# Four-layer HGRN2 / attention / DeltaNet trunk: wide value projection, output transposes off TensorE, joins set apart, norm in pieces

## The chip, the cores and the metric

The kernel runs on one core of a Trainium2 chip. The metric is the device time of one execution in microseconds (us). A profiled execution was taken beside the timed runs; every duration below comes from it. Engines are named as in the profile: PE is TensorE (matmuls; PEld its weight loads), DVE is VectorE, ACT is ScalarE, POOL is GpSimd, SP is the engine whose DMA queue carries nearly all transfers.

## What is computed

A trunk of four layers over 1024 tokens with 1024 features. Each layer normalises x, shifts and scales it by a conditioning vector, projects it, runs a token mixer, gates the result and adds its output projection to x:

```python
for i in range(DEPTH):                      # 4 layers
    shift, scale, gate = split(c @ ada_w[i] + ada_b[i])
    h = rmsnorm(x, norm_g[i]) * (1.0 + scale) + shift
    y = (hgrn2_mixer, swa_mixer, gdn_mixer)[i % 3](h, ...)   # layers 0 and 3 are HGRN2
    x = x + gate * y

def hgrn2_mixer(h, ...):                    # 8 heads of 128
    q, f_pre, i_, z = split(h @ w_in)       # i_ is the value v
    log_f = log(lb + (1 - lb) * sigmoid(f_pre));  k = (1 - lb) * sigmoid(-f_pre);  q = silu(q)
    o = rmsnorm(hgrn2_scan(q, k, i_, log_f), onorm_g)
    return (o * silu(z)) @ w_out

def swa_mixer(h, ...):                      # 16 query heads of 64, 4 key/value heads, window 128
    q, k, v, z = split(h @ w_in);  q, k = rope(rmsnorm(q)), rope(rmsnorm(k))
    return (softmax_with_sink(q @ k.T, window) @ v * silu(z)) @ w_out

def gdn_mixer(h, ...):                      # 16 value heads of 128, 8 query/key heads
    qkv, z, a, b = split(h @ w_in);  q, k, v = split(silu(causal_conv(qkv)))
    u = solve(I + A, ...)                   # per chunk of 64 tokens, unit lower triangular
    return (rmsnorm(scan(...), onorm_g) * silu(z)) @ w_out
```

Everything is fp32. The kernel splits each operand of a projection into a high and a low part and takes three matmuls for each product (high x high, high x low, low x high).

## The kernel before

**Layout.** x is kept feature-major (128 features in the partitions, 8 blocks of them) in two halves of 512 tokens, each 2 MB, in two "x" slots of SBUF. The normed h is kept as hhi and hlo for each half in four "h" slots. A projection whose result is feature-major (`proj_ps` and `outp_ps` in the profile) holds a 128x128 piece of weight in PE and moves 512 tokens past it. One whose result is token-major (`projt_ps`: the values of HGRN2 and q, k, v of the attention layer) holds 128 tokens of h and moves 256 columns of the weight. All go through `mm3`, the three matmuls L204, L205 and L206.

**Weights.** `load_w` issues a 256 KB load on SP's queue into one of 3 raw buffers (L177), casts it to w_hi on ACT (L179) and subtracts to w_lo on DVE (L180), with 4 buffers each.

**Order.** The mixers are written as generators that yield cost numbers. `weave` takes pieces from several streams in the proportion of their costs: the mixing of a head beside the projections of the next one. A scheduler then orders the instructions of each engine by priority; `burst` and `tied` give a group of small matmuls a high priority so that it stands together. Each engine executes its list in that order, so an instruction that waits holds up everything behind it on its engine.

**HGRN2 (layers 0 and 3).** `proj_v` gives the values of two heads at a time, 256 wide. `mix` works for each head and half: products of levels 1, 3 and 5 (`lev_ps`, L1040 for the first two, L1087 for the last), transposes of k (L1104), a scan over four chunks (`o_ps`, `s_ps`), a norm (L1132 on DVE), four PE transposes back to feature-major (`ot_ps`, L1136), the product with the gate silu(z) (L1139 on DVE) and a store to `od` in DRAM. The diagonal 32x32 blocks are copied by POOL (L1081), the others by ACT (L1090). The last head stays in SBUF. Then `out_load` and `out_mm` form the output projection from `od`.

**Attention (layer 1).** Keys and values are projected first, then one group of four query heads after another while the group before is mixed: scores, softmax, transposes of the probabilities (L1368), products with the values (L1374), which follow the transposes of each block of 128 keys.

**DeltaNet (layer 2).** `proj_kq` and `proj_v` pass through a causal convolution: two ACT reads of the PSUM result (L644 copy, L648 scale), three DVE taps (L650), a tanh. `inverse` builds the inverse of the triangular matrices: 16x16 blocks on DVE, then four *joins*, groups of small matmuls into `z_ps` (L811, L819 to L821, L828, L836), each of which waits for the copies of the one before. `scan` and `finish` follow; `finish` brings the outputs to feature-major with a 32x32-block transpose on DVE (L859) and four stores of 64 KB that put the blocks in place (L862).

**Between layers.** `norm_stats` and `norm_apply` make h for the next layer, half by half: per feature block n_t on DVE (L504), hhi on ACT (L505), hlo on DVE (L506). In the attention and DeltaNet layers, x is written to DRAM (`spill_x`, L127) after its norm and read back (`fill_x`, L132) before the output projection, both on SP's queue, 2 MB each; in the HGRN2 layers it stays in its slots.

## Time and profile before

| what | value |
|---|---|
| timed runs | 2688.74, 2692.27 and 2692.0 us; median 2692.0 us |
| the profiled execution | 2695.95 us, span 2694.2 us |
| PE busy | 2609.7 us (97%) |
| DVE busy | 2010.2 us (75%) |
| ACT busy | 1272.9 us (47%) |
| POOL busy | 136.7 us (5%) |
| DMA | 273.29 MB, 101 GB/s over the span |

Busy time of an engine is the union of its instructions' spans; the recorded length of a matmul (about 400 ns for 128x512) overlaps that of the next, so what a matmul costs in a row of matmuls is the distance between two starts. In a row of the profile stand the line, engine, operation, the tile written and the tiles read, the shape and the count; "idle before" is how long the engine had stood still and what released it.

### The profile page before, as it was taken

Reading aid. Unit: us, or ns where it says so; the run is one execution under the profiler, and the core shown is the slowest. Engines: PE = TensorE matmul, PEld = TensorE weight load, DVE = VectorE, ACT = ScalarE, POOL = GpSimd, SP = SyncE. Lnnn points to the kernel's source line nnn. Section 1 sums busy time; section 2 is a strip of 40 time slices with the busy share of each in tenths; the row PEclk is TensorE's granted clock in tenths of the full one; section 3 lists DMA queues with packets and bytes.
Section 4 is the critical chain, followed back from the end, with each engine's and each line's share of the span. In section 5 each row is a group of like instructions: output and inputs, shape, how many; then the busy total and the mean of one; then the engine's idle time right before and its main releaser. Section 6 shows DMA issues by size and latency. Waiting matters only on the chain.

```text
span 2694.2 us, 51458 instructions
## 1 busy us (share of the span) xinstructions
PE 2609.7 (97%) x18927; PEld 2102.4 (78%) x18927; DVE 2010.2 (75%) x5619; ACT 1272.9 (47%) x3268; POOL 136.7 (5%) x352
## 2 busy tenths in 40 slices
PE   8999999999999999999999999999999999999998
PEld 4878878778878777677877777777788878787877
DVE  6776766788687877777988888989876766656575
ACT  4333333444454655454556556666644433333342
POOL 0000100000000000001001101100000000000000
PEclk9999999999999999999999999999999999999999
DMA  6332222344223252333343333333584221111133
GB/s 241 92 93 84 68 79 72 110 137 157 59 87 103 75 158 91 114 98 84 102 115 99 96 105 100 94 97 82 179 254 132 71 60 37 56 51 43 49 118 115
DMA packets 361490, 273.29 MB, mean 101 GB/s; under 512 B 70499, under 2 KB 294166, under 8 KB 361238
## 3 DMA queue, kind: packets, MB, share of 16 engines
q1 hardware_dynamic: 360950, 268.96, 33.9%
q8 instruction: 149, 2.44, 0.4%
q14 instruction: 103, 0.84, 0.1%
q0 software_dynamic: 288, 1.05, 0.1%
HBM read 224.77 MB, written 45.15 MB: 100 GB/s over the span
## 4 chain that ended last, share of the span: by engine, by line
PE 71%; DVE 17%; DMA 5%; ACT 3%; issue 3%; SPq 1%; POOL 0%; DVEq 0%; ACTq 0%; POOLq 0%
PE proj_ps L206 10%; PE proj_ps L205 9%; PE proj_ps L204 9%; PE outp_ps L204 5%; PE outp_ps L205 5%; PE outp_ps L206 5%; DMA ada_w<-in_ada_w_dram 3%; PE projt_ps L204 3%; PE projt_ps L206 3%; PE projt_ps L205 3%; DVE w_lo L180 2%; DVE gd_tb L650 2%; PE pv_ps L1374 1%; DVE ada_acc L413 1%; PE w_ps L890 1%
## 5 line engine op out<-in xcount | busy, mean ns | idle before, releaser
L204 PE MATMUL proj_ps<-hhi,w_hi 128*128 128x512 f32 x1664 | 675.8, 406 | 6.1 <-ACT gd_tb L648 5.9
L206 PE MATMUL proj_ps<-hhi,w_lo 128*128 128x512 f32 x1664 | 679.9, 409 | 0.0
L205 PE MATMUL proj_ps<-hlo,w_hi 128*128 128x512 f32 x1664 | 671.2, 403 | 0.0
L204 PEld LDWEIGHTS proj_ps<-hhi,w_hi 128*128 128x128 f32 x1664 | 315.3, 190 | 59.4 <-ACT gd_tb L648 6.3
L205 PEld LDWEIGHTS proj_ps<-hlo,w_hi 128*128 128x128 f32 x1664 | 314.7, 189 | 59.0 <-issue 2.4
L206 PEld LDWEIGHTS proj_ps<-hhi,w_lo 128*128 128x128 f32 x1664 | 315.0, 189 | 56.1 <-issue 1.0
L179 ACT CAST w_hi<-w_raw 128x512 fp32r<-128x512 f32 x332 | 202.0, 611 | 303.3 <-PE proj_ps L205 188.1
L180 DVE TENSOR_TENSOR w_lo<-w_raw,w_hi 128x512 fp32r<-128x512 f32 x332 | 223.1, 674 | 155.2 <-ACT w_hi L179 129.1
L205 PE MATMUL projt_ps<-w_lo,hhi 128*128 128x256 f32 x896 | 258.7, 291 | 4.7 <-DVE w_lo L180 4.7
L204 PE MATMUL projt_ps<-w_hi,hhi 128*128 128x256 f32 x896 | 257.8, 290 | 0.6 <-ACT w_hi L179 0.6
L206 PE MATMUL projt_ps<-w_hi,hlo 128*128 128x256 f32 x896 | 256.8, 290 | 0.0
L204 PE MATMUL outp_ps<-o_hi,w_hi 128*128 128x512 f32 x576 | 229.2, 400 | 4.7 <-ACT o_hi L1200 3.4
L205 PE MATMUL outp_ps<-o_lo,w_hi 128*128 128x512 f32 x576 | 229.4, 399 | 0.0
L206 PE MATMUL outp_ps<-o_hi,w_lo 128*128 128x512 f32 x576 | 226.8, 396 | 0.7 <-DVE w_lo L183 0.7
L205 PEld LDWEIGHTS projt_ps<-w_lo,hhi 128*128 128x128 f32 x896 | 171.1, 192 | 8.1 <-DVE w_lo L180 6.0
L204 PEld LDWEIGHTS projt_ps<-w_hi,hhi 128*128 128x128 f32 x896 | 171.1, 192 | 3.7 <-ACT w_hi L179 1.0
L206 PEld LDWEIGHTS projt_ps<-w_hi,hlo 128*128 128x128 f32 x896 | 170.8, 192 | 2.4 <-issue 1.0
L650 DVE SCALAR_TENSOR_TENSOR gd_tb<-gd_xs,taps,gd_tb 128x512 f32<-128x512 f32 x192 | 145.2, 756 | 28.3 <-ACT gd_tb L648 19.7
L182 ACT ACTIVATE w_hi<-w_raw,par 128x512 fp32r<-128x512 f32 (+1 forms) x136 | 94.3, 698 | 137.0 <-PE outp_ps L205 89.2
L204 PEld LDWEIGHTS outp_ps<-o_hi,w_hi 128*128 128x128 f32 x576 | 108.8, 189 | 29.1 <-ACT o_hi L1200 4.9
L413 DVE SCALAR_TENSOR_TENSOR ada_acc<-ada_w,par,ada_acc 128x512 f32<-128x512 f32 x140 | 104.8, 749 | 33.4 <-DMA ada_w<-in_ada_w_dram 32.5
L206 PEld LDWEIGHTS outp_ps<-o_hi,w_lo 128*128 128x128 f32 x576 | 108.7, 189 | 23.5 <-DVE w_lo L183 1.3
(398 smaller groups left out, 4894.8 us busy)
## 6 DMA issues: line engine op xcount, KB each, us to landing
ada_w<-in_ada_w_dram SPq DMA_DIRECT2D x160, 256.0 KB, 2.8
w_raw<-in_hg_in_w_dram SPq DMA_DIRECT2D x136, 256.0 KB, 2.8
w_raw<-in_gd_in_w_dram SPq DMA_DIRECT2D x108, 256.0 KB, 3.0
o_in<-od SPq DMA_DIRECT2D x72, 256.0 KB, 3.2
w_raw<-in_gd_out_w_dram SPq DMA_DIRECT2D x64, 256.0 KB, 2.9
w_raw<-in_sw_in_w_dram SPq DMA_DIRECT2D x48, 256.0 KB, 2.9
w_raw<-in_hg_out_w_dram SPq DMA_DIRECT2D x40, 256.0 KB, 2.8
ada_w<-in_ada_w_dram SPq DMA_DIRECT2D x8, 1024.0 KB, 9.2
```

What stands on the lines that cost most here:

```text
L179: nc.scalar.copy(hi, raw)
L180: nc.vector.tensor_tensor(lo, raw, hi.bitcast(F32), ALU.subtract)
L182: nc.scalar.activation(hi, raw, AF.Copy, scale=scale)
L204: mm(out, a[0], b[0], start=start, stop=False)
L205: mm(out, a[0], b[1], start=False, stop=False)
L206: mm(out, a[1], b[0], start=False, stop=stop)
L413: self.nc.vector.scalar_tensor_tensor(acc, w, c, acc, ALU.mult, ALU.add)
L650: nc.vector.scalar_tensor_tensor(y, xs[:, j:j + HT], w(j), y, ALU.mult, ALU.add)
L890: nc.tensor.matmul(po[:, hd[a]], dd["u"][a, hf][:, cs], rhs, start=True, stop=True)
L1374: nc.tensor.matmul(po[a * 64:(a + 1) * 64], vg[:, n + 1 - nkb + b, :], p4[:, :, a, :], start=b == 0, stop=b == nkb - 1)
```

## The change

1. **Values of HGRN2, 512 wide.** `proj_v` now runs in two series (values 0 to 511 and 512 to 1023), each over all eight blocks of 128 tokens with `proj_wide`: 128 tokens of h are held and 512 columns of weight move past. The 8 weight pieces of a series are held together, four of them in new buffers. The values lie in the two "x" slots, so x is now spilled and filled in the HGRN2 layers too.
2. **Outputs of HGRN2.** For heads 0 to 6 the four PE transposes are replaced by a 32x32-block transpose on DVE, four rearranging stores of 64 KB to a new DRAM buffer `pd`, a load of 256 KB and the product with the gate (`gate`), which is issued at level 3 of the next half or head and is followed by the store to `od`.
3. **Level 5 products.** 16 matmuls in four column groups of 32 and at most 64 wide, in place of 12 in three groups up to 96 wide; the diagonal copies move from POOL to ACT, and the other copies become four for three.
4. **Joins.** Each join goes through `apart`: it is issued behind the projection matmul that was written last before it. The costs of the joins in `weave` rise from 900 or 1300 to 2200.
5. **Norm in pieces.** `norm_apply` is a generator; the second half of it (`self.last`) is drained at the start of the next layer. In the DeltaNet layer it is drained in pieces of 4 behind the taps of the first convolutions, and `hold` places the next convolution's copy behind them; n_t lies in PSUM. The early part of that layer also covers z of units 1 and 2 for the first half of the tokens.
6. **Attention.** v and the first q come first and k later; the four value products of a block are one `tied` group.
7. **Queues.** `spill_x` and `fill_x` issue on GpSimd's DMA queue; the final stores use the "h" slots.

```diff
-        self.nc.sync.dma_start(self.xd.rearrange("(k p) t -> p k t", p=P)[:, :, sl], self.x[hf])
+        self.nc.gpsimd.dma_start(self.xd.rearrange("(k p) t -> p k t", p=P)[:, :, sl], self.x[hf])
...
+    def apart(self, mms):
+
+        with self.tc.issue_after(self.mm.ins):
+            self.tied(mms)
...
+    def load_wide(self, w, c0, pool):
+
+        return [self.load_w(w[:, k, c0:c0 + HT], None, (None, pool)[k % 2]) for k in range(KT)]
...
     def norm_apply(self, i, hf, rb):
...
-            t = self.np.tile([P, HT], F32, name="n_t", tag="n_t", bufs=NB["n_t"])
+            t = self.psum("lev", "n_t", 2)
...
+            self.piece = nc.scalar.activation(hhi[:, k, :], t, AF.Identity, bias=S)
             nc.vector.scalar_tensor_tensor(hlo[:, k, :], t, S, hhi[:, k, :].bitcast(F32), ALU.add, ALU.subtract)
+            yield 1
...
-            nc.scalar.copy(xs[:, 3:], ps)
+            with self.tc.issue_after(self.hold.ins) if self.hold else nullcontext():
+                nc.scalar.copy(xs[:, 3:], ps)
...
+            self.piece = None
+            with self.tc.issue_after(last.ins):
+                drain(take(self.last, self.parts))
+            self.hold = self.piece
...
             z = bank("z_ps", 64)
-            self.tied([lambda g=g, q=q: nc.tensor.matmul(z[q, g % 8, :], uv[lo, g, up], Z[lo, g, :], start=True, stop=True)
+            self.apart([lambda g=g, q=q: nc.tensor.matmul(z[q, g % 8, :], uv[lo, g, up], Z[lo, g, :], start=True, stop=True)
                        for n in range(8) for g, q in ((n, up), (n + 8, lo))])
...
-            yield 900
+            yield 2200
...
+            yield from self.proj_wide(self.load_wide(w_in, 2 * D + m * HT, mp), ev, range(2 * NC))
...
+        def gate():
+
+            h, hf, z = pend.pop()
+            rows = (slice(h * P, (h + 1) * P), slice(hf * HT, (hf + 1) * HT))
+            t = tl("tmp")
+            nc.sync.dma_start(t, self.pd[rows])
+            nc.vector.tensor_tensor(v4(z, "c b"), v4(t, "b c"), v4(z, "c b"), ALU.mult)
+            nc.sync.dma_start(od[rows], z)
...
-                            nc.gpsimd.tensor_copy(at[gs, :, gs], A[gs].rearrange("p (c t) -> p c t", c=NC))
+                            nc.scalar.copy(at[gs, :, gs], A[gs].rearrange("p (c t) -> p c t", c=NC))
...
+                        self.tied([lambda c=c, m=m: mm(c, *m) for c in range(NC) for m in (
+                            (0, 3, slice(6, 7), slice(3, 4)), (0, 0, slice(0, 4, 3), slice(1, 3)),
+                            (1, 1, slice(1, 5, 3), slice(2, 4)), (2, 2, slice(2, 3), slice(3, 4)))])
...
+                    if l == 3 and pend:
+                        gate()
...
+                    nc.vector.tensor_tensor(v4(on, "b c"), v4(po, "c b"), r[:, :, None, None].to_broadcast([P, NC, 4, 32]), ALU.mult)
+                    ob = tl("tmp")
+                    nc.vector.transpose(ob, on)
+                    dst = self.pd[h * P:(h + 1) * P, hf * HT:(hf + 1) * HT].rearrange("(b q) (a t) -> a q b t", b=4, a=4)
+                    for a in range(4):
+                        nc.sync.dma_start(dst[a], ob[a * 32:(a + 1) * 32].rearrange("q (b t) -> q b t", b=4))
+                    pend.append((h, hf, d["zs", hf]))
...
         for h in range(H - 1):
...
+            gs = {0: [(0, "z")], 1: [], H - 2: [(h, "z"), (h + 1, "qfz")]}.get(h, [(h, "z")])
+            if h < H - 2:
+                gs.append((h + 1, "qfz" if h == 0 else "qf"))
+            g, tot = chain(*[proj(x, ds[x], p) for x, p in gs]), 10400 * sum(len(p) for _, p in gs)
+            if h == 1:
+                g, tot = chain(g, proj_v(1)), tot + 41600
+            weave(self.tc, (mix(h, ds[h]), 16000, 0, 1, PRH), (g, tot, 0, 1, 0), (take(side, ns), ns, 0, 1, 0))
...
+    def proj_wide(self, ws, evac, tts):
+
+        for tt in tts:
+            ps = self.proj_ps("projw_ps")
+            hf, ts = tt // 4, slice((tt % 4) * P, (tt % 4 + 1) * P)
+            for k in range(KT):
+                self.mm3(ps, (self.hhi[hf][:, k, ts], self.hlo[hf][:, k, ts]), ws[k], k == 0, k == KT - 1)
```

**ScalarE at the passage from the attention layer to the DeltaNet layer.** hhi is the high part of the normed h, gd_xs and gd_tb are the first convolution's copy and scale of a projection result, w_hi is a weight cast. Before:

```order
739 L505 ACTIVATE hhi<-n_t,mod 128x512
740 L179 CAST w_hi<-w_raw 128x512
741 L505 ACTIVATE hhi<-n_t,mod 128x512
742 L179 CAST w_hi<-w_raw 128x512
743 L505 ACTIVATE hhi<-n_t,mod 128x512 x2
744 L179 CAST w_hi<-w_raw 128x512
745 L505 ACTIVATE hhi<-n_t,mod 128x512 x2
746 L644 COPY gd_xs<-proj_ps 128x512
747 L648 ACTIVATE gd_tb<-proj_ps,taps 128x512
```

And with the change:

```order
762 L186 CAST w_hi<-w_raw 128x512 x3
763 L655 COPY gd_xs<-proj_ps 128x512
764 L659 ACTIVATE gd_tb<-proj_ps,taps 128x512
765 L565 CAST gd_wab<-w_raw 128x8x32
766 L186 CAST w_hi<-w_raw 128x512
767 L602 ACTIVATE gd_tmp<-gd_tmp 128x16
768 L667 ACTIVATE gd_tb<-gd_tb 128x512
769 L186 CAST w_hi<-w_raw 128x512
770 L514 ACTIVATE hhi<-n_t,mod 128x512 x2
```

The eight hhi of the second half stood ahead of the first convolution's copy; they now stand behind its first scale, two at a time.

**VectorE around a gate, a middle head of layer 0, with the change.** L1173 is the block transpose, L1056 the product with the gate, which reads what the load from `pd` brought; hg_S is the scan's state, w_lo a weight's low part.

```order
881 L1173 STREAM_TRANSPOSE hg_tmp<-hg_tmp 128x512
882 L1161 SCALAR_TENSOR_TENSOR hg_S<-hg_S,hg_F,s_ps 128x128
883 L1019 TENSOR_TENSOR hg_zs<-proj_ps,hg_tmp 128x512
884 L187 TENSOR_TENSOR w_lo<-w_raw,w_hi 128x512
885 L424 SCALAR_TENSOR_TENSOR ada_acc<-ada_w,par,ada_acc 128x512
886 L992 TENSOR_TENSOR hg_q<-proj_ps,hg_tmp 128x16x32
887 L1161 SCALAR_TENSOR_TENSOR hg_S<-hg_S,hg_F,s_ps 128x128
888 L424 SCALAR_TENSOR_TENSOR ada_acc<-ada_w,par,ada_acc 128x512
889 L1056 TENSOR_TENSOR hg_zs<-hg_tmp,hg_zs 128x512
890 L187 TENSOR_TENSOR w_lo<-w_raw,w_hi 128x512
891 L1166 TENSOR_SCALAR hg_ms<-hg_ssq 128x4
```

Seven instructions stand between the transpose of one half and its gate here. Of the 28 gates, 12 stand 5 to 9 rows behind their transpose and 16 stand 16 to 91 rows behind.

**TensorE at the third join of the fifth unit of DeltaNet.** L828 (now L842) is the join; it needs the copies made of the second join (L821, now L835), whose last row stands just ahead. Before, 4 projection matmuls stood between the two:

```order
7577 L821 MATMUL z_ps<-gd_Z,gd_Uc 32x32
7578 L906 MATMUL w_ps<-gd_wg,gd_uq 128x128
7579 L206 MATMUL proj_ps<-hhi,w_lo 128x512
7580 L204 MATMUL proj_ps<-hhi,w_hi 128x512
7581 L205 MATMUL proj_ps<-hlo,w_hi 128x512
7582 L206 MATMUL proj_ps<-hhi,w_lo 128x512
7583 L906 MATMUL w_ps<-gd_wg,gd_uq 128x128
7584 L828 MATMUL z_ps<-gd_Z,gd_uq 64x64 x16
7585 L204 MATMUL proj_ps<-hhi,w_hi 128x512
```

With the change:

```order
7110 L835 MATMUL z_ps<-gd_Z,gd_Uc 32x32
7111 L674 MATMUL vtr_ps<-ident,gd_tb 128x128 x4
7112 L217 MATMUL proj_ps<-hhi,w_lo 128x512
7113 L215 MATMUL proj_ps<-hhi,w_hi 128x512
7114 L216 MATMUL proj_ps<-hlo,w_hi 128x512
7115 L842 MATMUL z_ps<-gd_Z,gd_uq 64x64 x16
7116 L217 MATMUL proj_ps<-hhi,w_lo 128x512
```

Here the join moved no further off: three projection matmuls stand ahead of it. In the eight units the matmuls between second and third join were 4, 6, 10, 3, 4, 4, 6, 3; they are 4, 4, 18, 18, 3, 3, 12, 4.

More of the change, by code (lines that the diff above doesn't have):

```diff
@@ L1 @@
 import math
[L2 removed]
+from contextlib import ExitStack, nullcontext
 import numpy as np
@@ L1150, in hgrn2 @@
         ds = [dict() for _ in range(H)]
+        drain(self.last)
         gv = proj_v(0)
-        self.early(chain(proj(0, ds[0], "qf", (0,)), take(gv, 8)))
+        self.early(chain(proj(0, ds[0], "qf", (0,)), take(gv, 16)))
+        self.spill_x(1)
         drain(chain(gv, proj(0, ds[0], "qf", (1,))))
@@ L1261, in rotate @@
             nc.vector.tensor_tensor(b4[:, :, :, 32:64], p4[:, :, :, 0:32], bc(sg, slice(32, 64)), ALU.mult)
+            out = a if out is None else out
             nc.vector.tensor_tensor(out, a, b, ALU.add)
+            return out
         def sumsq(ps, out):
@@ L1457, in trunk @@
                     k.open_norm()
-                k.norm(nxt, hf)
-                if nxt % 3 and hf == 0:
+                a = k.norm_apply(nxt, hf, k.norm_stats(hf))
+                if hf == 0:
+                    drain(a)
                     k.spill_x(0)
-                if hf == 1:
+                else:
+                    k.last = a
                     k.nst.close()
```

228 lines of the change are left out of this document (115 added, 113 removed).

## The prediction, before the changed kernel was run

> **What bounds the kernel now.** I read the page's busy times first, then PE's waits, then the timeline at the places that the diff touches.
>
> ```profile
> span 2694.2 us, 51458 instructions
> PE 2609.7 (97%) x18927; PEld 2102.4 (78%) x18927; DVE 2010.2 (75%) x5619; ACT 1272.9 (47%) x3268; POOL 136.7 (5%) x352
> ...
> PE 71%; DVE 17%; DMA 5%; ACT 3%; issue 3%; SPq 1%; POOL 0%; DVEq 0%; ACTq 0%; POOLq 0%
> ```
>
> PE is busy 97% of the span and stands still for 2694.2 - 2609.7 = 84.5 us. So time can come from two places only: fewer or cheaper matmuls, or a part of these 84.5 us. PE's waits, the longest at places the change touches:
>
> ```profile
> PE lev_ps L1040 <- DVE hg_X L1063: 6.8, 19, 1.8
> PE z_ps L828 <- DVE gd_uq L823: 6.6, 7, 1.6
> PE proj_ps L204 <- ACT gd_tb L648: 5.9, 1, 5.9
> PE ot_ps L1136 <- DVE hg_tmp L1132: 5.6, 11, 1.3
> PE projt_ps L205 <- DVE w_lo L180: 4.7, 5, 1.4
> ```
>
> (total us, times, longest.) No wait is large, so most of a gain must be matmul time. The price of a matmul is the step from start to start, here for two kinds:
>
> ```profile
> 1028.91 0.39 PE L204 MATMUL outp_ps<-o_hi,w_hi 128*128 128x512 f32 x1
> 1029.14 0.39 PE L205 MATMUL outp_ps<-o_lo,w_hi 128*128 128x512 f32 x1
> ...
> 640.11 0.28 PE L204 MATMUL projt_ps<-w_hi,hhi 128*128 128x256 f32 x1
> 640.23 0.28 PE L205 MATMUL projt_ps<-w_lo,hhi 128*128 128x256 f32 x1
> ```
>
> 0.227 us for 512 columns and 0.120 us for 256, each as the mean over the rows that follow.
>
> **The change, part by part.**
>
> *Wide values.* 1536 matmuls of 256 columns become 768 of 512: 1536 x 0.120 - 768 x 0.227 = 184.3 - 174.3 = **-10 us**, all of it on PE. Bounds: 0 (if the long form pays something here that it doesn't in the output projection) and -10. The Trainium skill, "TensorE: Matmul & The Clock Gate", section "Back-to-back issue gap", makes an isolated matmul cost N / 2.4 ns plus a fixed 2.5 ns; by that the halved count would save only an estimated 768 x 2.5 ns = 1.9 us. The rows above give a fixed part of 2 x 0.120 - 0.227 = 0.013 us, five times as much, so this trace goes against it.
>
> *Outputs.* 28 groups of four transposes leave PE:
>
> ```profile
> 185.58 0.60 PE L1136 MATMUL ot_ps<-ident,hg_tmp 128*128 128x128 f32 x4
> 186.01 0.39 PE L1114 MATMUL o_ps<-hg_S,hg_qf 128*128 128x128 f32 x2
> 186.24 0.39 PE L1115 MATMUL o_ps<-hg_v,hg_at 128*128 128x128 f32 x2
> 186.38 0.48 PE L204 MATMUL proj_ps<-hhi,w_hi 128*128 128x512 f32 x1
> 186.69 0.40 PE L205 MATMUL proj_ps<-hlo,w_hi 128*128 128x512 f32 x1
> 186.93 0.40 PE L206 MATMUL proj_ps<-hhi,w_lo 128*128 128x512 f32 x1
> ```
>
> A group takes 186.01 - 185.58 = 0.43 us: 28 x 0.43 = **-12 us**. The waits in front of them (5.6 us, above) go with 7 of 8 groups: **-5 us**; to nothing at the worst, if the matmul that is next in line waits for the same norm.
>
> *Changes between kinds.* After a group of other matmuls the first 512-wide product takes 0.31 to 0.34 us to the next start (186.38 to 186.69) rather than 0.23 to 0.24: about 0.09 us for each return. The orders of PE have 1028 such returns before and 916 now (26 fewer behind ot_ps, 18 behind o_ps, 14 behind kk_ps, 9 or fewer behind each of the others): 112 x 0.09 = **-10 us**. Bounds: -20, should the way into a group cost as much as the way out, and -5, if only the ot_ps groups and their neighbours count.
>
> *Level 5 products.*
>
> ```profile
> 120.37 0.47 PE L206 MATMUL proj_ps<-hhi,w_lo 128*128 128x512 f32 x1
> 120.78 0.85 PE L1087 MATMUL lev_ps<-hg_X,hg_kg 128*32 128x96 f32 x24
> 121.56 0.50 PE L204 MATMUL proj_ps<-hhi,w_hi 128*128 128x512 f32 x1
> ```
>
> The 12 matmuls of the code are 24 in the profile, 64 wide in the mean, and take 0.78 us. Two 128-wide o_ps ones take 0.23 us (186.01 to 186.24), so 24 of half that width in turn would take 1.38: the column groups run beside each other, and the 96-wide ones set the pace, 8 x 0.115 x 96 / 128 = 0.69 us and 0.1 of starting. Four groups of at most 64 give 8 x 0.0575 + 0.13 = 0.59 us: 32 x (0.78 - 0.59) = **-6 us**, bounds -13 (half the time) and +4 (32 passes in turn in place of 24 where four groups don't overlap better than three). The diagonal copies go to ACT:
>
> ```profile
> L1081 POOL COPY hg_at<-hg_A 32x128 f32<-32x128 f32 x128 | 59.9, 468 | 940.3 <-DVE hg_F L1093 556.9 <-DVE hg_A L1076 360.9 <-DVE hg_F L1098 16.8
> L1090 ACT COPY hg_at<-lev_ps 32x128 f32<-32x128 f32 x32 | 8.2, 256 | 0.4
> ```
>
> 128 x 0.26 = 33 us more for ACT, hidden: ACT is busy 47%. Without that cover it would delay the scan, by four copies, 1 us a half.
>
> *Attention.* The value products of a block in one series save returns (counted above) and let two pieces run beside each other: **-2 us** (0 to -4). The waits on w_lo (4.7 us, above) come with 256-wide products, of which fewer than half remain, and the attention layer starts with v and q in place of k and v: **-2 us** (0 to -4).
>
> *Into DeltaNet.* ACT's first convolution copy stood behind hhi's:
>
> ```profile
> 1131.57 1.38 ACT L505 ACTIVATE hhi<-n_t,mod 128x512 fp32r<-128x512 f32 x2 [0.69 <-DVE n_t L504]
> ...
> 1134.82 1.38 ACT L505 ACTIVATE hhi<-n_t,mod 128x512 fp32r<-128x512 f32 x2 [1.07 <-DVE n_t L504]
> 1136.10 0.57 ACT L644 COPY gd_xs<-proj_ps 128x512 f32<-128x512 f32 x1
> 1136.57 0.69 ACT L648 ACTIVATE gd_tb<-proj_ps,taps 128x512 f32<-128x512 f32 x1
> ...
> 1137.31 0.80 PE L204 MATMUL proj_ps<-hhi,w_hi 128*128 128x512 f32 x1 [5.86 <-ACT gd_tb L648]
> ...
> 1140.89 0.59 PE L206 MATMUL proj_ps<-hhi,w_lo 128*128 128x512 f32 x1
> ```
>
> PE waits 5.86 us for a free PSUM bank and then makes eight steps in 3.58 us (1137.31 to 1140.89), 0.45 each rather than 0.23: 1.8 us more. In the new order of ACT the copy stands ahead of these hhi, and eight groups of products of the first half (8 x 24 x 0.227 = 43.6 us) cover the rest of the norm: **-8 us** (5.9 + 1.8 + a little of the next wait; bounds 0, if the pieces only move the wait to the second half, and -10).
>
> *Joins.* One third join of eight had no wait; the other seven cost 0.94 us each. In the new order 3 units have 12 to 18 matmuls ahead of it (2.7 to 4.1 us), one of them the unit without a wait, and five keep 3 or 4: **-2 us** (0 to -5; 0.5 lost if five joins find one product fewer).
>
> *What it costs.* (a) x goes to DRAM in the HGRN2 layers as well, four 2 MB writes or reads a layer, and all on GpSimd's queue. In layer 0 the first write falls into the start:
>
> ```profile
> 20.00:25.00 5.00, 5.00 (x12) 0.97 (x11) 4.51 (x19) 0.00 (x0) 0.75 (x2) 1.00 1.11 346
> 25.00:30.00 5.00, 5.00 (x18) 1.63 (x17) 2.72 (x6) 2.13 (x4) 0.46 (x1) 1.00 1.06 392
> ...
> xd<-x SPq DMA_DIRECT2D x4, 2048.0 KB, 8.0
> rope_sw_qnorm<-cg_sw_qnorm POOLq DMA_DIRECT2D x1, 512.0 KB, 7.1
> rq<-rope_sw_qnorm SPq DMA_DIRECT2D x1, 512.0 KB, 3.8
> ```
>
> The DMA engines are full there (share 1.06 to 1.11, 346 to 392 GB/s; last two columns), so 2.1 MB more may cost 2.1 MB / 390 GB/s = 5.4 us; half of the loads there are of use only later: **+3 us** (0 to 5.4). Elsewhere 2 MB on GpSimd's queue take 8.0 x 7.1 / 3.8 = 15 us, or 4 x 7.1 = 28 us if the rate doesn't grow. x of half 1 must be out before its slot takes values, 124 products (28 us) later; a fill has about 200 products (46 us): hidden by both.
>
> (b) DVE gets 28 transposes of 0.70 us (20 us of 684 us idle) and 28 gates that wait for DRAM:
>
> ```profile
> L859 DVE STREAM_TRANSPOSE gd_of<-gd_of 128x512 f32<-128x512 f32 x32 | 22.5, 704 | 0.1
> ...
> L862 SPq DMA_DIRECT2D od<-gd_of x128: 302/432/1777, 1305.2 to 1986.0; - x128
> ...
> od<-gd_of SPq DMA_DIRECT2D x128, 64.0 KB, 1.8
> o_in<-od SPq DMA_DIRECT2D x72, 256.0 KB, 3.2
> ```
>
> The same four stores are made in DeltaNet. Round trip: three issues of 0.43, the fourth store's 1.8, the load's 3.2 = 6.3 us. 12 of the 28 gates stand 5 to 9 rows behind their transpose, some 3.3 us at 0.2 to 0.75 each, so DVE would stand still 12 x 3 = 36 us. Behind such a gate stand a weight's low part (four are in store, 5.4 us of products each) and the norm of the next half, for which nobody hurries: a fifth reaches PE, **+8 us** (0 to 36).
>
> (c) Heads 2 to 5 of each layer now have three projection units beside their mixing, not four:
>
> ```profile
> 303.00:365.00 62.00, 59.40 (x600) 52.25 (x599) 40.69 (x134) 20.36 (x51) 3.74 (x8) 1.00 0.28 82
> 365.00:428.00 63.00, 62.40 (x527) 48.89 (x526) 42.26 (x134) 21.60 (x55) 4.38 (x8) 1.00 0.25 73
> ```
>
> (us, then busy time of PE, PEld, DVE, ACT and POOL with counts.) A head takes 62.5 us, DVE 41.5 of them. A unit is 48 products, 10.9 us: 52 us a head, DVE about 41 with the transposes, 79% in place of 66%. The waits on hg_X (6.8 us) should rise: **+5 us** (0 to 30).
>
> **Sum:** -10 - 12 - 5 - 10 - 6 - 2 - 2 - 8 - 2 = -57, + 3 + 8 + 5 = +16: **-41 us**. Against the profiled execution, 2695.95, that is 2655; the timed median lies 4 us lower, so **2651 us**.
>
> **Rivals.**
> - *Dense heads.* The mixing chain through DVE sets the pace in the eight heads with three units. For it: PE waits for hg_X 19 times already, more often than for anything else above. Against it: 11 us of DVE idle remain a head. At 4 us a head beyond my 5: +27, 2678 us.
> - *Larger gains.* Returns at twice 0.09 (-10), level 5 at -13, no cost of gates or density (-13): 2621 us.
> - *Slower: the gates' round trip.* SP issues in order, and the stores stand among weight loads that wait for buffers (a store's issue took up to 1.78 us above). With T for the round trip, DVE stands still 12 x (T - 3.3) + 16 x (T - 7) us; passed on in full this eats the 41 + 8 us from T = (49 + 39.6 + 112) / 28 = 7.2 us on, passed on by half from T = 8.9 us on; at 9 us in full, 100 us, 2702 us. Against it: what stands behind the gates is mostly not urgent.
> - *GpSimd's queue too slow.* If 2 MB took 40 us there, the two values' slots would be 12 us late in layers 0 and 3: 2675 us. The Trainium skill, "SBUF — State Buffer", section "Who interferes with whom", warns that a GpSimd-issued DMA is starved by certain DVE copies; its figures (620 to 3100 ns, factor 5) would make of 8.0 us the estimated 40. The row above shows a factor of 1.9 beside SP's.
> - *It doesn't do what it says.* The joins stay close in five of eight units, by the order; and if wide products brought nothing: 2661 us.
>
> **How the numbers follow.** My sum 0.52 (2632 to 2670), dense heads 0.18, larger gains 0.13, gates 0.09, GpSimd 0.05, nothing from the wide form 0.03. The range 2618 to 2688 leaves out the gates and half of the larger gains. 0.2%, some 5 us, is what a measurement of this kernel can tell from no change: faster (below 2686) 0.86, within 0.05, slower 0.09.
>
> **What would show it.** Right: PE busy falls by 35 to 45 us and its share stays near 97%; no wait on gd_tb above 2 us at the DeltaNet entry; wide values at steps of 0.227; DVE waits on the gate's load of 2 to 4 us, 12 times; POOL's 2 MB at 15 to 28 us. Wrong: waits of PE on hg_X or w_lo that sum to over 30 us, gate waits over 5 us, or PE waiting for x.

## The result

The changed kernel takes 2713.88 us (median of 4 runs, 2712.96 to 2715.92) against 2692.14 us: a ratio of 1.0084 (95% interval 1.0072 to 1.0097), 22 us slower. The forecast was 2651, range 2618 to 2688. One execution of e14 below (2818.72 us, granted clock 0.845) fell in a slow state of the chip and is left out of its ratio.

The page of the changed kernel, its busy times and two of its DMA queues:

```profile
span 2712.3 us, 50574 instructions
...
PE 2595.1 (96%) x18303; PEld 2055.8 (76%) x18303; DVE 2013.6 (74%) x5645; ACT 1318.7 (49%) x3464; POOL 92.5 (3%) x240
...
q1 hardware_dynamic: 379254, 272.11, 34.6%
q0 software_dynamic: 8736, 34.60, 3.5%
```

PE's busy time fell by 14.6 us only, and its idle time rose from 84.5 to 2712.3 - 2595.1 = 117.2 us. So the kernel does less work and waits more. What it waits for (total us, times, longest):

```profile
PE lev_ps L1074 <- DVE hg_X L1097: 11.1, 15, 4.2
...
PE pt_ps L1438 <- DVE sw_sm L1432: 5.0, 3, 2.8
...
PE ktr_ps L674 <- DVE gd_k L668: 4.4, 2, 3.7
PE n_ps L494 <- DVE n_acc L491: 4.3, 1, 4.3
PE n_rb L501 <- DVE n_sq L499: 4.1, 2, 3.7
```

Before, nothing but the DeltaNet entry reached 4 us at a time; now single waits of 2.8 to 4.3 us stand in these five places, most at a passage between layers or at a head's end. By stages, from the start to the first layer's second norm, then layer 0, then the last part of attention up to the norm for DeltaNet; first before, then after (us, busy time and count of PE, PEld, DVE, ACT, POOL, granted clock, DMA share, GB/s):

```profile
0.00:61.60 61.60, 52.34 (x194) 23.93 (x194) 35.94 (x127) 27.45 (x48) 4.43 (x44) 0.97 0.73 259
61.60:588.00 526.40, 512.69 (x4523) 423.44 (x4523) 371.90 (x1120) 194.51 (x447) 32.40 (x69) 0.99 0.31 92
...
1053.50:1121.90 68.40, 64.43 (x323) 47.27 (x321) 55.32 (x131) 39.21 (x88) 1.31 (x4) 1.00 0.36 108
```

```profile
0.00:67.30 67.30, 56.77 (x205) 26.39 (x205) 37.79 (x129) 29.99 (x51) 6.21 (x46) 1.00 0.78 289
67.30:594.00 526.70, 503.96 (x4080) 397.91 (x4081) 368.78 (x1110) 208.82 (x522) 3.00 (x4) 0.98 0.39 117
...
1064.40:1143.50 79.10, 70.58 (x330) 52.57 (x330) 56.02 (x130) 37.08 (x84) 2.07 (x5) 0.90 0.25 75
```

The start is 5.7 us longer. Layer 0 has 8.7 us less PE work and is no shorter: the gain went into waits. The passage to DeltaNet is 10.7 us longer, and PE's clock was granted at 0.90 there; e5 and e12 below show that nearly all of this part is not the transfers'. Behind the wait of 4.31 us that ends at 585.71 us the clock was granted at 0.50 (the third column from the end), and PE's steps are longer for a while:

```profile
587.00:592.00 5.00, 5.00 (x14) 3.94 (x14) 3.57 (x14) 0.09 (x1) 0.00 (x0) 0.50 0.37 107
...
587.65 0.63 PE L215 MATMUL outp_ps<-o_hi,w_hi 128*128 128x512 f32 x1
588.08 0.63 PE L216 MATMUL outp_ps<-o_lo,w_hi 128*128 128x512 f32 x1
```

The step is 0.43 us, not 0.23, for twelve steps: some 2.4 us more, on top of the wait.

**What the waits stand next to.** At 573 us GpSimd issues the write of x, 2 MB. The timelines of POOL, ACT and PE in the changed kernel, one after the other:

```profile
573.17 0.89 POOL L129 DMA_DIRECT2D xd<-x  x1 [82.41 <-DVE x L544]
...
575.91 0.63 ACT L490 ACTIVATE n_sq<-x 128x512 f32<-128x512 f32 x1 [0.63 <-DVE n_acc L491]
582.32 0.72 ACT L189 ACTIVATE w_hi<-w_raw,par 128x512 fp32r<-128x512 f32 x1 [5.78 <-DMA w_raw<-in_hg_out_w_dram]
582.95 0.61 ACT L490 ACTIVATE n_sq<-x 128x512 f32<-128x512 f32 x1
...
585.71 1.51 PE L494 MATMUL n_ps<-ones,n_acc 128*128 128x1 f32 x8 [4.31 <-DVE n_acc L491]
```

The weight loads issued from 573 to 582 us, their time from issue to landing:

```profile
DMA to landing us min/median/max: 7.2/7.6/8.2
```

The three weight loads land 7.2 to 8.2 us after their issue, where the median of such loads is 2.8. ACT's next cast waits 5.78 us for one of them, and in ACT's list the rest of the norm's squares stand behind that cast; PE waits 4.31 us for their sum. PE would soon have needed that weight too: it had one product left before it.

Late loads are not new. In the kernel before, a load on SP's queue right behind the write of x took as long (SP's timeline, then the landing of the first of these loads):

```profile
1045.85 0.37 SPq L127 DMA_DIRECT2D xd<-x  x1
1046.90 3.10 SPq L177 DMA_DIRECT2D w_raw<-in_sw_out_w_dram  x3
...
DMA to landing us min/median/max: 7.8/7.8/7.8
```

What PE waits for because of it is what changed.

### The profile page after: what moved, and what is told of

Same layout as the page of the kernel before. It is cut to its first block, busy times and chain, and to the rows that moved or that the text cites. A ratio compares the mean times of both kernels' runs of the same rounds, so it can differ in the third digit from the quotient of the medians.

```text
span 2712.3 us, 50574 instructions
## 1 busy us (share of the span) xinstructions
PE 2595.1 (96%) x18303; PEld 2055.8 (76%) x18303; DVE 2013.6 (74%) x5645; ACT 1318.7 (49%) x3464; POOL 92.5 (3%) x240
## 4 chain that ended last, share of the span: by engine, by line
PE 52%; issue 18%; DVE 16%; DMA 9%; ACT 4%; SPq 1%; POOL 0%; DVEq 0%; ACTq 0%; POOLq 0%
PE proj_ps L217 8%; PE proj_ps L215 7%; PE proj_ps L216 7%; PE outp_ps L215 4%; PE outp_ps L217 4%; PE outp_ps L216 4%; DMA ada_w<-in_ada_w_dram 3%; DVE gd_tb L661 2%; PE projw_ps L217 2%; PE projw_ps L216 2%; PE projw_ps L215 2%; DVE w_lo L187 2%; DMA w_raw<-in_hg_in_w_dram 2%; PE w_ps L904 1%; PE lev_ps L1074 1%
## 5 line engine op out<-in xcount | busy, mean ns | idle before, releaser
L217 PE MATMUL proj_ps<-hhi,w_lo 128*128 128x512 f32 x1664 | 672.2, 404 | 0.0
L187 DVE TENSOR_TENSOR w_lo<-w_raw,w_hi 128x512 fp32r<-128x512 f32 x352 | 236.1, 675 | 173.9 <-ACT w_hi L186 172.7
L186 ACT CAST w_hi<-w_raw 128x512 fp32r<-128x512 f32 x352 | 214.3, 612 | 283.8 <-PE proj_ps L216 151.7
L190 DVE SCALAR_TENSOR_TENSOR w_lo<-w_raw,par,w_hi 128x512 fp32r<-128x512 f32 (+1 forms) x136 | 97.0, 714 | 47.1 <-ACT w_hi L189 46.0
L216 PEld LDWEIGHTS outp_ps<-o_lo,w_hi 128*128 128x128 f32 x576 | 110.8, 192 | 24.3 <-DVE o_lo L1262 1.6
L216 PE MATMUL projt_ps<-w_lo,hhi 128*128 128x256 f32 x384 | 111.2, 292 | 2.2 <-DVE w_lo L187 2.1
L215 PE MATMUL projt_ps<-w_hi,hhi 128*128 128x256 f32 x384 | 111.2, 292 | 1.8 <-ACT w_hi L186 1.8
L217 PE MATMUL projt_ps<-w_hi,hlo 128*128 128x256 f32 x384 | 111.3, 292 | 0.0
L215 PE MATMUL projw_ps<-w_hi,hhi 128*128 128x512 f32 x256 | 101.4, 403 | 1.7 <-ACT w_hi L186 1.2
```

What stands on the lines that cost most here:

```text
L186: nc.scalar.copy(hi, raw)
L187: nc.vector.tensor_tensor(lo, raw, hi.bitcast(F32), ALU.subtract)
L190: nc.vector.scalar_tensor_tensor(lo, raw, scale, hi.bitcast(F32), ALU.mult, ALU.subtract)
L215: mm(out, a[0], b[0], start=start, stop=False)
L216: mm(out, a[0], b[1], start=False, stop=False)
L217: self.mm = mm(out, a[1], b[0], start=False, stop=stop)
```

## Experiments

Ratios are to runs of the kernel before on the same chip, with 95% intervals; 0.001 is 2.7 us.

### The transfers of x

**e1: x on SP's queue.** All 16 transfers, nothing else.

```diff
-        self.nc.gpsimd.dma_start(self.xd.rearrange(...)[:, :, sl], self.x[hf])
+        self.nc.sync.dma_start(self.xd.rearrange(...)[:, :, sl], self.x[hf])
```

(and `fill_x` likewise)

> The changed kernel, but x is written and read on SP's queue again, all 16 transfers of 2 MB. Theory T (transfers): the loss comes from the 2 MB transfers, which run beside the weight loads on a queue of their own; the loads land 3 to 5 us late and ScalarE, which executes in order, stands before them, with the norm's or the mixing's work behind it. With the transfers in SP's own line the order leaves room for them: waits of PE at 501, 586 and 1064 us (4.2, 4.3 and 3.7 us) shrink below 1.5 us, and the time falls by 8 to 20 us, to 2694 to 2706 us. Theory O (order at the seams): the norm in pieces, the gates and the denser heads make the waits, the queue is innocent: within 4 us of 2714. Theory N (number): it is that there are 16 transfers and not 8, whatever the queue: within 6 us of 2714, with the waits at the same places.

Measured: 2682.13 us, 0.9979 (0.9965 to 0.9993). One word in each of two lines is worth 0.0105, 28 us: theory T's direction, more than its 20. ACT and SP of this run at the same norm:

```profile
559.99 0.37 SPq L129 DMA_DIRECT2D xd<-x  x1
...
564.12 0.63 ACT L490 ACTIVATE n_sq<-x 128x512 f32<-128x512 f32 x1 [0.50 <-DVE n_acc L491]
565.38 0.63 ACT L490 ACTIVATE n_sq<-x 128x512 f32<-128x512 f32 x1 [0.63 <-DVE n_acc L491]
568.94 2.16 ACT L189 ACTIVATE w_hi<-w_raw,par 128x512 fp32r<-128x512 f32 x3 [2.92 <-DMA w_raw<-in_hg_out_w_dram]
```

The weight loads are late here too (6.7 us for the one issued at 563.5 us), but ACT's list has the squares ahead of the casts. The two kernels differ in the queue alone, so the order of ACT's list follows from it; I take it that the scheduler counts a transfer against loads in its own queue and not against those in another, which the rows agree with but no run shows apart from the queue. PE's waits of 4.2, 4.3 and 3.7 us are gone. In their place stand waits for late weights themselves; PE's idle time falls from 117.2 to 98.8 us, and the same matmuls are busy for 14.7 us less. Two of these waits:

```profile
571.62 0.50 PE L217 MATMUL outp_ps<-o_hi,w_lo 128*128 128x512 f32 x1 [1.17 <-DVE w_lo L190]
...
586.01 0.50 PE L217 MATMUL outp_ps<-o_hi,w_lo 128*128 128x512 f32 x1 [3.23 <-DVE w_lo L190]
```

**e2: the kernel before, its 8 transfers on GpSimd's queue.** The same two lines of the kernel before, the other way.

> The kernel before, with its 8 transfers of x on GpSimd's queue and nothing else changed. Theory T: they collide with weight loads as in the changed kernel; PE gets new waits of 2 to 4 us at four or more of the eight and the time rises by 5 to 12 us, to 2697 to 2704. Theories O and N: within 4 us of 2692.

Measured: 2703.68 us, 1.0056 (1.0035 to 1.0076): 15 us for 8 transfers, as theory T said or a little more. The new waits stand at places where the changed kernel has them too:

```profile
PE n_rb L493 <- DVE n_sq L491: 4.8, 2, 3.2
PE n_ps L486 <- DVE n_acc L483: 4.6, 2, 4.2
...
PE z_ps L811 <- ACT gd_Tc L793: 3.8, 1, 3.8
```

**e5: pieces on SP's queue.** Each transfer becomes eight of 256 KB; `load_w` first issues the next piece, behind the `mm3` written last.

```diff
+        x = self.x[hf]
+        self.pq += [lambda k=k: self.nc.sync.dma_start(self.xd[k * P:(k + 1) * P, sl], x[:, k, :]) for k in range(KT)]
...
+    def step(self):                       # called by load_w; xslot() issues what is left
+        if self.pq:
+            with self.tc.issue_after(self.mm.ins) if self.mm else nullcontext():
+                self.pq.pop(0)()
```

> The changed kernel with x on SP's queue, and each 2 MB transfer cut into eight of 256 KB, which are issued one at each weight load, behind the projection matmul written last. Theory T2: even on SP's queue a whole 2 MB transfer holds up the weight load behind it (waits of PE on w_lo or w_hi of 1.2 to 3.2 us at 571, 586, 1046, 1052 and 1126 us in that run); cut up, they shrink and the time falls by 4 to 12 us below the whole transfers' 2682, to 2670 to 2678. Rival: what is left doesn't come from transfers, or 128 issues cost SP as much: within 4 us of 2682.

Measured: 2670.52 us, 0.9930 (0.9914 to 0.9946): another 13 us. A whole transfer on SP's queue still holds up what follows. By stages, layer 0 and the passage to DeltaNet of this run:

```profile
64.20:570.60 506.40, 495.08 (x4079) 391.50 (x4079) 368.02 (x1110) 209.46 (x522) 0.31 (x1) 1.00 0.40 122
...
1031.00:1108.50 77.50, 68.99 (x331) 51.91 (x330) 56.21 (x131) 38.35 (x87) 1.28 (x4) 0.91 0.30 88
```

Layer 0 takes 506.4 us in place of 526.7: the gain that had gone into waits is back. The passage still takes 77.5 us, against 79.1 in the changed kernel and 68.4 before, so most of its loss has another cause (see e12).

**e10: the kernel before with pieces.** The same edit of the kernel before.

> The kernel before, with its 8 transfers of x cut into pieces of 256 KB, one at each weight load, on SP's queue. Theory T2: a whole transfer costs some 0.8 us each on SP's queue; the time falls by 4 to 8 us, a ratio of 0.997 to 0.9985. Rival: in the kernel before the order already gave them room: within 2 us of it.

Measured: 2685.08 us, 0.9976 (0.9966 to 0.9986), 6.5 us faster, within theory T2. Its 8 whole transfers cost 0.8 us each, the 16 of e1 as much each. On GpSimd's queue a whole transfer costs 2.6 us against pieces on SP's (the changed kernel against e5, 41 us for 16), and 2.7 us in the kernel before (e2 against e10, 21.5 us for 8).

**e13: pieces, on GpSimd's queue.** e5 with `gpsimd` for `sync` in both lists of pieces (the writes' here, the reads' likewise).

```diff
-        self.pq += [lambda k=k: self.nc.sync.dma_start(self.xd[k * P:(k + 1) * P, sl], x[:, k, :]) for k in range(KT)]
+        self.pq += [lambda k=k: self.nc.gpsimd.dma_start(self.xd[k * P:(k + 1) * P, sl], x[:, k, :]) for k in range(KT)]
```

> The changed kernel with x in pieces of 256 KB, one at each weight load, but on GpSimd's queue. Theory S (size): a weight load is held up only by what is under way, and 256 KB are soon through; as on SP's queue with pieces: a ratio of 0.993. Theory Q (queue): transfers on a queue that the order treats as apart collide all the same, 41 us for 16 whole ones; with pieces at least a third of the loss stays: 0.998 to 1.004.

Measured: 2697.23 us, 1.0022 (1.0012 to 1.0032). Both the size and the queue count: on GpSimd's queue the pieces are 17 us faster than the whole transfers (1.0084), and with the same pieces GpSimd's queue is 25 us slower than SP's. The eight pieces of a read go out on GpSimd's queue 0.5 us apart, within 3.8 us; on SP's they take 5 to 23 us, with one to nine other transfers of that queue in between. The writes go out at a similar pace in both for the most part. Two of e13's longest waits of PE, 5.4 us at 505.5 and 3.1 us at 965.5, end 11 to 13 us behind the first piece of a read. That the burst makes them is what I infer; no run changes the pace alone. The issues and their landing, e13 first, then e5:

```profile
xd<-x POOLq DMA_DIRECT2D x64, 256.0 KB, 2.9
x<-xd POOLq DMA_DIRECT2D x64, 256.0 KB, 6.0
```

```profile
xd<-x SPq DMA_DIRECT2D x64, 256.0 KB, 2.3
x<-xd SPq DMA_DIRECT2D x64, 256.0 KB, 4.3
```

### HGRN2's parts

**e4: outputs through PE transposes** in the changed kernel (transfers on GpSimd's queue), heads 0 to 6 as before.

```diff
-                    nc.vector.transpose(ob, on)
-                    for a in range(4):
-                        nc.sync.dma_start(dst[a], ob[a * 32:(a + 1) * 32].rearrange("q (b t) -> q b t", b=4))
-                    pend.append((h, hf, d["zs", hf]))
+                    nc.tensor.transpose(pt[:, cs], on[:, cs], self.ident)   # four of them
+                nc.vector.tensor_tensor(of, pt, d["zs", hf], ALU.mult)
+                    nc.sync.dma_start(od[h * P:(h + 1) * P, hf * HT:(hf + 1) * HT], of)
```

> The changed kernel, but the outputs of HGRN2's heads 0 to 6 go through PE transposes and the product with the gate as before; no stores to and loads from the second buffer. Prediction's step: the transposes cost PE 12 us and their waits and returns 5 to 8, the gates cost 8: the time rises by 5 to 12 us, to 2719 to 2726. Theory G (gates): VectorE's waits at the gates take more than that; the time falls by 5 to 15 us, to 2699 to 2709.

Measured: 2728.74 us, 1.0137 (1.0110 to 1.0163): 14 us slower, so the outputs' edit gains that much. The gates cost almost nothing. Their instruction in the changed kernel, and what VectorE waited for there:

```profile
L1056 DVE TENSOR_TENSOR hg_zs<-hg_tmp,hg_zs x28: 678/684/694, 162.4 to 2610.9; 128x512 f32<-128x512 f32 x28
its engine sat idle before it (us, times) until:
  DMA hg_tmp<-pd: 4.0, 5
```

4.0 us in 5 of 28, where the prediction had 36 us in 12.

**e8: level 5 as before**, on e1: the 12 matmuls in three column groups, diagonals on GpSimd.

```diff
-                        self.tied([lambda c=c, m=m: mm(c, *m) for c in range(NC) for m in (...)])
+                        with self.burst():
+                          for c in range(NC):
+                            for g in range(3):
...
-                            nc.scalar.copy(at[gs, :, gs], A[gs]...)
+                            nc.gpsimd.tensor_copy(at[gs, :, gs], A[gs]...)
```

> The changed kernel with x on SP's queue, and the level 5 products and the diagonal copies as before (12 matmuls up to 96 wide in three column groups, diagonals on GpSimd). By the prediction's step the new form saves 6 us (bounds -13 and +4): the time rises by 4 to 9 us above 2682. Rival: the copies that moved to ScalarE delay the scan and eat it: within 3 us.

Measured: 2689.86 us, 0.9995 (0.9985 to 1.0006) against e1's 0.9979: 4 us slower, though the two intervals still overlap. The step was 6; direction and size agree with it as far as these runs can tell.

**e11: the wide products cut in two**, on e9 (below): the same weights, buffers and stores, 256 columns at a time.

```diff
+            for n in range(2):
+                ns = slice(n * 256, (n + 1) * 256)
                 for k in range(KT):
-                    self.mm3(ps, (...), ws[k], k == 0, k == KT - 1)
+                    self.mm3(ps[:, ns], (...), [a[:, ns] for a in ws[k]], k == 0, k == KT - 1)
```

> As the kernel with pieces and tied joins, but each 512-wide value product is made as two of 256 columns, with the same weights, buffers and stores: 1536 matmuls in place of 768. By the prediction's step of 0.013 us each, 10 us slower than that kernel. Rival, a fixed part of 2.5 ns a matmul: 2 us slower.

Measured: 2679.01 us, 0.9955 (0.9943 to 0.9967) against 0.9927: 7.5 us slower, where the rows gave 10 and the fixed part of 2.5 ns gave 2. The Trainium skill's figure ("TensorE: Matmul & The Clock Gate", section "Back-to-back issue gap") is for an isolated matmul and too small in this stream; the trace's is the nearer.

### Outside HGRN2

**e3: the norm at once**, in the changed kernel.

```diff
-                    k.last = a
+                    drain(a)
```

> The changed kernel, but the norm of the second half is applied at once when the layer before ends, not at the start of the next layer nor in pieces behind the convolutions. Theory O: most of the loss of 11 us at the passage from attention to DeltaNet comes from the pieces; it goes and the time falls to about 2703. Theory T: the passage is lost to weights that land late beside x's transfer at 1137 us; the time stays within 5 us of 2714 or rises to 2719, since ScalarE's first convolution copy stands behind the norm again.

Measured: 2714.15 us, 1.0088 (1.0064 to 1.0111): no difference. The pieces brought no gain and made no loss that shows beside the transfers.

**e6: joins tied, with their old costs**, on e1.

```diff
-            self.apart([lambda g=g, z=z, p_=p_, b_=b_: nc.tensor.matmul(...)
-            yield 2200
+            self.tied([lambda g=g, z=z, p_=p_, b_=b_: nc.tensor.matmul(...)
+            yield 900
...
-        weave(self.tc, (inverse(0, ds[0]), 34300, 0, 0.85, 100),
+        weave(self.tc, (inverse(0, ds[0]), 28000, 0, 0.8, 100),
```

> The changed kernel with x on SP's queue, and the joins tied as before with their old costs (900 and 1300) instead of set apart. By the prediction's step the joins bring 2 us, so the time rises by 0 to 4 us above 2682. Rival J: the joins with the higher costs lose time (DeltaNet took 4.5 us longer than before in that run): it falls by 3 to 8 us, to 2674 to 2679.

Measured: 2677.77 us, 0.9958 (0.9942 to 0.9973), 6 us faster than e1, with intervals that just overlap: rival J. **e9** puts the edits of e5 and e6 together:

> The changed kernel with x in pieces of 256 KB on SP's queue and the joins tied with their old costs: the two that gained, together. If both gains add (13 us for the pieces, 6 for the joins, against the whole transfers on SP's queue at a ratio of 0.998): a ratio of 0.991, some 2665 to 2668 us. Rival: the joins' gain was that of another order around the transfers and is gone with the pieces: 0.993, as the pieces alone.

Measured: 2671.20 us, 0.9927 (0.9914 to 0.9940), the same as the pieces alone. So set apart or tied, the joins are level once the transfers are in pieces; what e6 gained belonged to the order around whole transfers. The prediction's 2 us gain isn't there.

**e7: attention as before**, on e1 (k and v first, value products behind their transposes).

```diff
-        self.early(chain(proj_v(0), proj_q(0, ds[0], (0, 1))))
+        self.early(kv(0))
...
-                self.tied([...value products of all key blocks...])
+                    for a in range(2):
+                        nc.tensor.matmul(po[a * 64:(a + 1) * 64], vg[:, n + 1 - nkb + b, :], p4[:, :, a, :], start=b == 0, stop=b == nkb - 1)
```

> The changed kernel with x on SP's queue, and the attention layer as before: k and v first, and each block's value products behind its own transposes. By the prediction's step (2 us for the series, 2 for the passage) the time rises by 2 to 5 us above 2682. Rival A: the series of value products makes PE wait for the last block's copy, and the layer takes 3.4 us more than before for it: the time falls by 2 to 8 us.

Measured: 2685.95 us, 0.9979 (0.9968 to 0.9990), equal to e1. **e15** undoes the same on e9:

> x in pieces on SP's queue, joins tied; HGRN2, the norm in pieces and DeltaNet as changed, attention's order and value products as before. If attention loses the 6 us: a ratio of 0.9905. If DeltaNet and its norm lose them: 0.993.

Measured: 2673.20 us, 0.9925 (0.9911 to 0.9938), equal to e9. Attention's edits are worth nothing either way.

**e12: the HGRN2 part alone.** Attention, DeltaNet, their norms and joins from the kernel before, except that n_t stays in PSUM as in the changed kernel; x in pieces on SP's queue. The whole edit is long (`swa`, `gdn` and their lists are those of the kernel before); its core, against e9:

```diff
-        self.early(chain(proj_kq(0, ds[0], ((0,),)), proj_z(1, ds[1], (0,)), proj_z(2, ds[2], (0,))), EV)
-        drain(self.last)
+        self.early(proj_kq(0, ds[0], ((0,),)), EV)
...
-        self.early(chain(proj_v(0), proj_q(0, ds[0], (0, 1))))
+        self.early(kv(0))
```

> The changed HGRN2 layers with the attention and DeltaNet layers, their norms and joins as they were before, and x in pieces on SP's queue. If the changes outside HGRN2 bring what the prediction gave them (12 us for attention, the passage into DeltaNet and the joins): 8 to 14 us slower than the kernel with pieces and tied joins. Theory S (those changes lose time at the seams, 13 us in the run with whole transfers): 3 to 10 us faster than it.

Measured: 2666.94 us, 0.9905 (0.9890 to 0.9919): 6 us faster than e9, theory S. Against the kernel before with the same pieces (0.9976) the HGRN2 part is worth 19 us. The passage to DeltaNet, e10 first, then e12, and PE's longest wait in e12's:

```profile
1046.10:1111.90 65.80, 62.35 (x316) 46.43 (x315) 54.30 (x124) 37.52 (x85) 1.31 (x4) 1.00 0.35 105
...
1042.10:1120.00 77.90, 69.84 (x328) 50.67 (x327) 56.12 (x130) 37.94 (x86) 1.28 (x4) 0.91 0.30 89
...
1056.26 0.27 PE L1417 MATMUL s_ps<-band,identb 128*128 128x256 bf16 x1 [2.63 <-DVE hlo L532]
```

It is 12 us longer, with attention's code as before and x in the same pieces. What e12 keeps of the change there is n_t in PSUM, in the two "lev" slots that attention's scores (s_ps) use as well; hlo's instruction is the one that reads n_t, and PE waits for it. The same wait of 2.6 us stands in the changed kernel and in e5, e9, e14 and e16, and in no kernel with n_t in SBUF. No run moves n_t alone, so this is the likely cause of a part and not shown; e1, e6 and e8 have n_t in PSUM without that wait, at 73.8 to 75.3 us.

**e14** has only DeltaNet and the norm ahead of it as before (the first of these two places, and the convolution without the norm's pieces):

```diff
-            with self.tc.issue_after(self.hold.ins) if self.hold else nullcontext():
-                nc.scalar.copy(xs[:, 3:], ps)
+            nc.scalar.copy(xs[:, 3:], ps)
...
-            with self.tc.issue_after(last.ins):
-                drain(take(self.last, self.parts))
```

> x in pieces on SP's queue; HGRN2 and attention as changed, DeltaNet and the norm ahead of it as before (joins tied). If DeltaNet and its norm in pieces lose the 6 us: a ratio of 0.9905, as the HGRN2 part alone. If attention loses them: 0.993, as all parts together.

Measured: 2664.42 us, 0.9902 (0.9888 to 0.9917). This is the lowest ratio of all, 26 us below the kernel before, and it says where the 6 us are: DeltaNet with its norm. **e16** and **e17** undo the two halves of that, each on e9: the norm in pieces, and the units projected early.

```diff
-                    k.last = a
+                    drain(a)
```

```diff
-        self.early(chain(proj_kq(0, ds[0], ((0,),)), proj_z(1, ds[1], (0,)), proj_z(2, ds[2], (0,))), EV)
+        self.early(proj_kq(0, ds[0], ((0,),)), EV)
```

> x in pieces on SP's queue, joins tied, the norm of the second half applied at once; the early z of units 1 and 2 stays. If the norm in pieces loses the 6 us: a ratio of 0.9902 to 0.991. If the early projections lose them: 0.992 to 0.9935. By the prediction's step (8 us gained by the pieces) it would be 0.9955.

> x in pieces on SP's queue, joins tied, the norm in pieces; the early part of DeltaNet covers only q, k and z of unit 0, as before, and z of the later units comes in the old order. If the early projections lose the 6 us: 0.9902 to 0.991. If the norm in pieces loses them: 0.992 or more, since less work then covers the pieces.

Measured: 2666.60 us, 0.9915 (0.9898 to 0.9932), and 2666.99 us, 0.9914 (0.9900 to 0.9928). Both lie between 0.9902 and 0.9927, within the uncertainty of either; which half loses stays open. Neither supports the step that gave the pieces 8 us.

## Why the prediction was wrong

The forecast was -41 us, the result +22: 63 us apart. In three parts, from the ratios:

| part | forecast, us | measured, us | from |
|---|---|---|---|
| HGRN2's edits, their returns, gates and density | about -25 | -19 | e12 against e10 |
| attention, DeltaNet, norm and joins, with their returns | about -19 | +7 | e5 against e12 |
| x: 16 transfers and their queue | +3 | +35 | changed kernel against e5 (41), less what the 8 of before cost (6.5, e10) |
| sum | -41 | +23 | |

(The forecast's 10 us for returns are split evenly over the first two rows.)

- **What failed first: "hidden by both".** It was priced at 3 us in all and cost 35. In step (a) of the costs I asked whether a 2 MB transfer on GpSimd's queue would itself be late, found 15 to 28 us against 28 to 46 us of slack, and called it hidden. It was even quicker:

```profile
xd<-x POOLq DMA_DIRECT2D x8, 2048.0 KB, 9.2
x<-xd POOLq DMA_DIRECT2D x8, 2048.0 KB, 9.6
```

The question left out was who else is in line: the weight loads beside it, and behind the weight load ACT, and behind ACT the norm or the mixing. I had asked it of the gates' wait, and not of a transfer that nobody waits for. The loads land late beside a 2 MB transfer on either queue (7.8 us before, 7.2 to 8.2 now); with the queue, what stood behind them in ACT's list changed. The Trainium skill states plainly that they share their way, in "DMA: Bandwidth & Descriptors", section "Issuing engines are not separate DMA queues": whatever engine starts a DMA, all run on the same 16 engines and interleave. The loads that land at 7.2 to 8.2 us agree.

- **The rival on GpSimd's queue** had the right suspect and the wrong mechanism. It let the values' slots come late at 40 us a transfer; they came at 9 to 10, and PE never waited for x. The rule of the Trainium skill beside it ("SBUF — State Buffer", section "Who interferes with whom"), that VectorE can starve a GpSimd-issued DMA, is not what happened: 9.2 us against 7.9 for the same writes in e1. Its advice, "Switch to HWDGE", which e1 follows with SP's queue (hardware_dynamic in the page above), helped for a reason that it doesn't give.

- **The start, +3**: the first write went out at 20.7 us, into the full DMA engines, since nothing on GpSimd held it back; the stage grew by 5.7 us. In e1 it stood on SP behind the start's loads, went out at 51.4 us, and the stage grew by 3.0. The bound of 5.4 nearly held.

- **Into DeltaNet, -8**: the convolution's wait did shrink, from 5.9 us to 3.3 in five parts, but another took its place, which the step did not name. Beside the write of x at 1137 us a weight comes late, and ACT and PE stand:

```profile
1147.74 0.62 ACT L186 CAST w_hi<-w_raw 128x512 fp32r<-128x512 f32 x1 [6.36 <-DMA w_raw<-in_gd_in_w_dram]
...
1154.72 0.52 PE L674 MATMUL ktr_ps<-ident,gd_k 128*128 128x128 f32 x3 [3.73 <-DVE gd_k L668]
```

Without that collision (e9, e14, e16, e17) the kernels with less of the DeltaNet edits are 3 to 7 us faster than e9, so the step's gain of 8 us isn't there by itself either; that the sign is the other way rests on e14, whose interval (0.9888 to 0.9917) barely meets e9's (0.9914 to 0.9940), and on e12 (0.9890 to 0.9919).

- **n_t in PSUM** had no term in the sum, though the change names it. In the kernels that have n_t there the passage to DeltaNet takes 74 to 82 us, in those that have it in SBUF (before, e2, e10) 66 to 69, whatever the queue and the pieces. Those kernels have the changed HGRN2 layers too, so how much of this n_t makes is open.

- **Wide values, -10**: 7.5 measured. **Outputs, -12 - 5, less +8 for the gates**, with some 3 us of returns: -12 forecast, -14 measured; the pieces were off in opposite ways, since the gates cost near nothing (4.0 us of VectorE's idle time against 36: the twelve nearest gates start 6.7 to 9.1 us behind their transpose, where I had counted 3.3 against a round trip of 6.3). **Level 5, -6**: 4. These steps, taken from rows of the same operation, held, level 5 with the doubt named at e8.

- **Attention, -4** and **joins, -2**: nothing measurable. **Density, +5**: not measured by itself, but the waits on hg_X, which should have risen from 6.8 us, sum to 5.7 in e5. The three undone parts of HGRN2 sum to 26 us, the HGRN2 part as a whole to 19; the 7 between them hold the density, the values' copies, the eight more transfers in pieces and what e12's passage to DeltaNet loses, not told apart.

- The rival that was slower (gates) named the wrong round trip, and its price was added up wrong: 100 us of VectorE's standing still, less the gains of 49, lie above the kernel before, at 2743 us, not above the forecast, at 2702. The one that fits, transfers that collide with loads, was not among the rivals with a price.

- **The signs** named for being wrong did not show: waits on hg_X sum to 11.1 us, the longest gate wait is 1.3 us, PE never waits for x. Of those for being right, wide steps of 0.227 us and gd_tb waits below 2 us came true, while PE's busy time fell by 14.6 us in place of 35 to 45. They looked at the parts that I had priced.

## What to carry to other kernels

Before a bulk transfer is moved to an idle engine's queue, list what else the DMA engines carry in those microseconds and which in-order engine waits for it: "nobody waits for this transfer" says nothing about those that share its way. Here an idle queue was worse than a busy one: the loads beside the transfer were late on both, and on the idle one an in-order engine's list had urgent work behind them. Cut such a transfer up and put the pieces in the loads' own line: 0.8 us a transfer came back even in the kernel before. And when a tile is moved to shared PSUM slots, look for who else takes turns there.

## What was not expected of the hardware

A 2 MB transfer on GpSimd's queue is nearly as fast as on SP's (9.2 and 9.6 us against 7.9 and 9.0). The prediction's factor of 1.9 came from two rows that were not alike: the transfer of 512 KB that took 7.1 us was issued at 22.8 us, into the full DMA engines of the start, and the one of 3.8 us at 629.7 us. And pieces on GpSimd's queue win back only a part of what the whole transfers lose there: 1.0022 against 1.0084 whole, and 0.9930 in pieces on SP's.
